# The top-k selection of a sparse-attention layer: a bound steered by counts in place of a search by bits

## The chip, the cores and the metric

The kernel runs on one core of a Trainium2 chip. A core has five engines with a queue each: TensorE (PE in the views, its weight loads PEld), VectorE (DVE), ScalarE (ACT), GpSimd (POOL) and SyncE (SP), which here issues all the DMA transfers. Each engine runs its own list of instructions in order and waits on semaphores for the others. The metric is the device time of one execution in microseconds, lower being better.

## The reference

The reference computes one decoder layer on 1024 tokens of width 1024 in float32. The part around the change is the sparse branch. For each query token t and each key position s it forms an index score, keeps the 256 highest-scored positions at or before t, and attends to those alone:

```python
dots = einsum('bqhd,bsd->bqhs', iq, ik) * IDX_DIM ** -0.5
score = einsum('bqh,bqhs->bqs', iw, relu(dots))        # 8 index heads
score = where(causal, score, NEG_INF)
_, idx = lax.top_k(score, 256)                         # ties: lowest position first
sel = c_kv[idx]                                        # then softmax attention, 8 heads, over sel
```

Beside it stand a projection of the input to all queries, keys and values, a sliding-window attention (8 heads), a cross attention over 256 memory tokens whose keys and values are two projections of the memory, a 4096-wide squared-ReLU network, and four layer norms. A token before position 256 has no more than 256 candidates, so it keeps them all and needs no selection.

## The kernel before

Tokens are handled in eight blocks of 128, a token to a partition. Every large product is made of three single-pass products of split operands: a value is rounded to a high part and the rest is kept as a low part, so each weight piece costs a rounding copy (`wh`, L156 on GpSimd, L158 on VectorE, L160 on ScalarE) and a subtraction (`wl`, L161) before TensorE can use it. `wload` loads and splits such pieces of 128x512, in a ring of four buffers each for raw, high and low.

Order of the stages: norm and transposition of the input, index queries and scores, then two things side by side, and then the attention of both branches, the output projection, the cross attention, the network and the final norm. The two things side by side are the ones that the change touches:

- The selection. Blocks 2 to 7 need one, with rows of 384 to 1024 scores (`sc`, 4224 columns over the six blocks). A score's bits are read as an ordered integer key of two 16-bit halves: `to_keys` makes the high keys as soon as a block's last index head is added (L584 to L597), and `search` finds the 256th largest key bit by bit, 15 steps on the high halves, then 16 on the low ones. In a step `look` counts a row's keys at or above the bound c, and `move` makes two one-column operations that halve the bracket (L665, L667). Blocks 2 to 5 are counted on VectorE (L584); blocks 6 and 7 on ScalarE, as a sum of signs (L680, with L684 and L687). The steps of the blocks are interleaved. Five passes of VectorE over each block (L733 to L737) then turn the threshold into a mask written over the scores, with a running sum that settles ties.
- The `fill` list: 53 units of TensorE work that need no selection, and seven that open the attention's memory and start its first loads. The first 36 are 18 units of projections of window and sparse queries and keys, mixed with 18 small ones (memory transposition, latent keys, the first memory keys); then come the memory keys (`mem_k`), the memory values (`mem_v`) and their product with the output weights (`mem_vo`). Memory weights are split on ScalarE, VectorE and GpSimd for the keys (`both`), on ScalarE and GpSimd alone for the values. A projection unit evicts its result on ScalarE (L393), splits it on GpSimd (L395, L396) and stores it (L398).

In the program text the whole selection stands ahead of the fill list. Earlier text has the higher priority; a planner orders each engine's list at compile time with estimated costs, so that fill units go between the steps of the selection where they are ready. `Pace` ties the fill matmuls to the last index-score matmuls by hand. At run time each list is fixed. The attention units that follow read the masks (L860), make probabilities (L863, L865), transpose and split them (`PT`, L768, L769) and multiply by the values (`VV`, L829, L830).

Of the kernel before, what the change touches and what calls it, by code (L numbers as in the profile page):

```python
# [21 lines left out]
P = 128  # L22
# [7 lines left out]
BUCKETS = 32  # L30
NOSYNC = mybir.DependencyInfo(mybir.DependencyClass.NoSync, mybir.DependencyReason.DATA)
# [3 lines left out]
def kernel(ctx: ExitStack, tc: tile.TileContext, x, mem, ln_emb_g, ln_emb_b, w_in, b_in,  # L35
# [240 lines left out]

    TW = 328
# [62 lines left out]
    bias_rows()  # L340
    st0.close()
# [217 lines left out]
    hi_k = {}  # L559
    HI = {7: (3, 0), 3: (7, 1024), 6: (4, 0), 4: (6, 896), 5: (2, 0), 2: (5, 768)}  # L560
    NQ = NB - 2
    cnt0, neg, flip, low, least, T_hi, base, need, t_lo = (
        p1.tile([P, NQ], F32, name=nm) for nm in ("cnt0", "neg", "flip", "low", "least", "T_hi", "base", "need", "t_lo"))

# [3 lines left out]
    def hi_half(n):  # L568
        mate, o = HI[n]
        if (n, mate) not in hi_k:  # L570
            hi_k[n, mate] = hi_k[mate, n] = p1.tile([P, 1536], I16, name="hi_k", tag="qs", bufs=4)
        hi_k[n] = hi_k[n, mate][:, o:o + (n + 1) * P]
        return hi_k[n]

    def col(t, n):
        return t[:, n - 2:n - 1]

    junk = {}

    def new_junk():  # L580
        junk["v"] = p1.tile([P, 1024], BF, name="junk", tag="r", bufs=3)

    def count(key, c, o, op=OP.is_ge):
        DVE.tensor_scalar(junk["v"][:, :key.shape[-1]], key, c, None, op0=op, op1=OP.add, accum_out=o)  # L584
# [3 lines left out]


    def to_keys(n):  # L590
        new_junk()
        count(halves(n, 1, I16), 0.0, col(cnt0, n))
        DVE.tensor_scalar(col(neg, n), col(cnt0, n), float(TOPK), -1.0, op0=OP.is_ge, op1=OP.add)
        DVE.tensor_scalar(col(flip, n), col(neg, n), 2.0, 1.0, op0=OP.mult, op1=OP.add)
        POOL.tensor_scalar(hi_half(n), halves(n, 1, I16), col(flip, n), col(neg, n), op0=OP.mult, op1=OP.add)
        DVE.tensor_scalar(col(least, n), col(neg, n), col(cnt0, n), float(TOPK), op0=OP.mult, op1=OP.add)
        DVE.tensor_scalar(col(low, n), col(neg, n), -65535.0, None, op0=OP.mult)  # L597

    def index_scores(j, qs):
        for e in range(2):  # L600
            h = 2 * j + e
            for n in (2, 4, 6, 3, 5, 7):
# [17 lines left out]
                if h == 7:  # L620
                    to_keys(n)
# [10 lines left out]

    SIGN = (NB - 1, NB - 2)
    lo_k = {}
    for tag, bufs, ns in (("ikh", 1, (7, 6)), ("ikl", 1, (5, 4, 3)), ("qs", 4, (2,))):
        t = p1.tile([P, sum(n + 1 for n in ns) * P], U16, name="lo_k", tag=tag, bufs=bufs)
        o = 0
        for n in ns:  # L640
            lo_k[n] = t[:, o:o + (n + 1) * P]
            o += (n + 1) * P
    new_junk()
    junk_a = p1.tile([P, 1024], BF, name="junk_a", tag="r", bufs=3)

    def srow(n):
        return sc[:, SCO[n]:SCO[n] + (n + 1) * P]

    class Counter:

        def __init__(self, n, key, least, out, bits):
            self.n, self.key, self.least, self.out, self.bits = n, key, least, out, bits
            self.c = self.small("c")
            DVE.memset(self.c, float(1 << bits - 1))

        def small(self, nm):
            return p1.tile([P, 1], F32, name=nm + str(self.n), bufs=2)

        def look(self):
            self.got = self.small("n")  # L660
            count(self.key, self.c, self.got)
# [78 lines left out]
    for unit, *args in fill:  # L740
        unit(*args)
# [680 lines left out]
```

## Time and profile before

| | |
|---|---|
| median of 3 runs | 1568.49 us (1567.64 to 1571.1) |
| the profiled execution | 1567.31 us, its span 1565.2 us |
| TensorE busy | 1436.3 us, 92% of the span |
| VectorE, GpSimd, ScalarE busy | 1166.9, 839.5, 797.0 us |
| mean granted TensorE clock | 0.966 |

The profile is one execution. Times inside it count from the first instruction, and the span ends with the last; the execution's own time is 2.1 us longer. Matmuls are pipelined, so a busy TensorE need not be at its peak, and the granted clock of a stretch says how fast it was let run. In a wait, the engine named last is the one whose work came last by the profile.

### The profile page before, as it was taken

To read this page: it belongs to the slowest core of one execution; us is meant where nothing else is said; L and a number is where in the kernel's file an instruction comes from. 1 tells how busy PE (TensorE), PEld (TensorE's weight loads), DVE (VectorE), ACT (ScalarE), POOL (GpSimd) and SP (SyncE) were. 2 spreads that over 40 slices of the span, in tenths; PEclk is the share of its full clock that TensorE was granted. 3 is DMA by queue.
4 is the path that set the end of the run, shared out by engine and by line. 5 is a ranking of instruction groups with operands and counts; after the bars stand their busy time and mean duration, and the time that the engine had idled before them with its cause. 6 is when DMAs were issued, how large, how long until landed. Compare 5 with 4: busy or idle time off the path is not lost. (4 is left out here: it accounts for less than half of the span.)

```text
span 1565.2 us, 22294 instructions
## 1 busy us (share of the span) xinstructions
PE 1436.3 (92%) x7190; PEld 1210.2 (77%) x7190; DVE 1166.9 (75%) x2442; ACT 797.0 (51%) x1665; POOL 839.5 (54%) x754
## 2 busy tenths in 40 slices
PE   5989997785998999899999979999999999999787
PEld 4877786764897988688888858888888877888676
DVE  8739899969786878985264495575544899988857
ACT  6336677673787875235334254545554533444422
POOL 6213855555556554755564675645444344453745
PEclk9999999896999999999999989999999999999999
DMA  6262444774649249623322133433333933420002
GB/s 218 72 163 71 135 135 139 234 249 108 199 144 247 95 135 290 181 94 114 109 73 90 41 108 122 136 107 126 117 126 114 389 110 109 148 69 1 27 28 107
DMA packets 139907, 206.63 MB, mean 132 GB/s; under 512 B 18055, under 2 KB 83086, under 8 KB 139790
## 3 DMA queue, kind: packets, MB, share of 16 engines
q1 hardware_dynamic: 139790, 205.21, 41.7%
q8 instruction: 57, 0.93, 0.3%
q14 instruction: 60, 0.49, 0.1%
HBM read 151.66 MB, written 52.45 MB: 130 GB/s over the span
## 5 line engine op out<-in xcount | busy, mean ns | idle before, releaser
L86 PE MATMUL b<-a,wh 128*128 128x512 f32 x1072 | 293.8, 396 | 9.0 <-DVE a L1077 8.2
L161 POOL TENSOR_TENSOR wl<-wr,wh 128x512 fp32r<-128x512 f32 x158 | 225.2, 1443 | 142.8 <-ACT wh L160 129.2
L86 PE MATMUL b<-wl,wh 128*128 128x512 f32 x1192 | 280.4, 395 | 15.1 <-POOL wl L1091 12.9
L86 PEld LDWEIGHTS b<-wl,wh 128*128 128x128 f32 x1192 | 226.1, 190 | 66.4 <-POOL wl L1091 15.8
L86 PEld LDWEIGHTS b<-a,wh 128*128 128x128 f32 x1072 | 203.7, 191 | 52.7 <-issue 9.0
L1091 POOL TENSOR_TENSOR wl<-a,wl 128x512 fp32r<-128x512 f32 x44 | 92.6, 2105 | 113.5 <-ACT wl L1090 109.1
L160 ACT ACTIVATE wh<-wr 128x512 fp32r<-128x512 f32 x136 | 81.3, 627 | 125.9 <-PE b L86 46.4
L1091 POOL TENSOR_TENSOR wh<-row,wh 128x512 fp32r<-128x512 f32 x72 | 97.9, 1366 | 84.4 <-ACT wh L1090 81.0
L86 PE MATMUL fill<-xT,wh 128*128 128x512 f32 (+1 forms) x416 | 125.5, 381 | 6.7 <-ACT wt L393 6.7
L86 PE MATMUL b<-wh,a 128*128 128x512 f32 (+1 forms) x416 | 120.9, 365 | 7.1 <-DVE a L761 5.3
L86 PE MATMUL b<-a,wl 128*128 128x512 f32 x400 | 120.7, 391 | 0.0
L1090 ACT ACTIVATE wh<-a 128x512 fp32r<-128x512 f32 x80 | 50.5, 631 | 115.2 <-PE b L86 83.8
L86 PEld LDWEIGHTS fill<-xT,wh 128*128 128x128 f32 x416 | 77.5, 192 | 22.7 <-ACT wt L393 8.2
L86 PEld LDWEIGHTS b<-wh,a 128*128 128x128 f32 x416 | 76.3, 191 | 21.0 <-DVE a L761 5.8
L1284 DVE TENSOR_TENSOR xr<-xr,b 128x512 f32<-128x512 f32 x132 | 81.6, 681 | 12.8 <-PE b L86 12.8
L86 PEld LDWEIGHTS b<-a,wl 128*128 128x128 f32 x400 | 75.2, 188 | 15.1
L1102 ACT ACTIVATE lt<-lt,colst 128x512 f32<-128x512 f32 x60 | 43.2, 722 | 73.7 <-DVE lt L1209 73.0
L86 PE MATMUL fill<-xT,wl 128*128 128x512 f32 (+1 forms) x208 | 78.8, 381 | 0.0
L769 DVE TENSOR_TENSOR PT<-tr,PT 128x512 fp32r<-128x512 f32 (+3 forms) x128 | 70.6, 576 | 9.0 <-ACT PT L768 8.7
L86 PE MATMUL b<-wl,a 128*128 128x512 f32 (+1 forms) x208 | 75.4, 365 | 1.7 <-POOL wl L161 1.7
L768 ACT ACTIVATE PT<-tr 128x512 fp32r<-128x512 f32 (+3 forms) x128 | 61.6, 507 | 26.1 <-PE tr L870 10.9
L1209 DVE TENSOR_TENSOR lt<-b,lt 128x512 f32<-128x512 f32 x80 | 53.2, 685 | 26.9 <-PE b L86 20.8
(328 smaller groups left out, 3664.2 us busy)
## 6 DMA issues: line engine op xcount, KB each, us to landing
row<-in_w_up_dram SPq DMA_DIRECT2D x32, 512.0 KB, 4.3
ff_d<-lt SPq DMA_DIRECT2D x28, 512.0 KB, 3.0
a<-in_w_down_dram SPq DMA_DIRECT2D x50, 256.0 KB, 5.4
a<-ff_d SPq DMA_DIRECT2D x46, 256.0 KB, 3.3
wr<-in_xa_wkv_dram SPq DMA_DIRECT2D x32, 256.0 KB, 3.9
wr<-in_w_o_dram SPq DMA_DIRECT2D x32, 256.0 KB, 3.1
wr<-in_xa_wq_dram SPq DMA_DIRECT2D x32, 256.0 KB, 3.0
wr<-vwo_d SPq DMA_DIRECT2D x32, 256.0 KB, 2.8
```

Source lines behind the costliest of these rows:

```text
L86: i = PE.matmul(o, a, b, start=start, stop=stop)
L160: ACT.activation(hs, raw, AF.Copy)
L161: lo[i % len(lo)].tensor_tensor(out=ls, in0=raw, in1=f(hs), op=OP.subtract)
L768: ACT.activation(PT[0], pt, AF.Copy)
L769: DVE.tensor_tensor(out=PT[1], in0=pt, in1=f(PT[0]), op=OP.subtract)
L1090: ACT.activation(hl[:, 0], raw, AF.Copy)
L1091: return lo.tensor_tensor(out=hl[:, 1], in0=raw, in1=f(hl[:, 0]), op=OP.subtract)
L1102: ACT.activation(c, src, AF.Relu, bias=colst[:, C_UP + col:C_UP + col + 1])
L1209: DVE.tensor_tensor(out=o, in0=a, in1=b, op=op)
L1284: DVE.tensor_tensor(out=xs, in0=xs, in1=p, op=op)
```

## The change

The search by bits is replaced, and where the selection stands in the text changes.

- `normal_bounds` computes once, for each row, the bound at which a normal distribution would have 251.5 scores above it, and the slope of that bound with the count.
- `Counter` and `Signer` take the place of `to_keys`: mean and variance of the first part of a row (at most 512 scores), a square root on GpSimd, and a first bound. Eight steps follow in place of 31. In each, the row's scores at or above the bound are counted in float32 (VectorE for blocks 2 to 5, ScalarE's signs for 6 and 7) and the bound moves by the miss times the slope times a weight from `PULL`.
- A last count marks the scores above the bound for all six blocks; marked scores are pushed far down and one instruction takes the eight largest of the rest. The needed one among them (the 256th less those counted) is the threshold, and the number of larger ones settles ties.
- A row whose count ended outside the eight is odd. The largest oddness of a partition goes by a transfer of 128 values into one row, VectorE takes its maximum, loads it into a register and branches: if any row is odd, all six blocks are done by bits on VectorE (`settle`), each instruction waiting for the one before it; if none is, that code is jumped over.
- The branch and the masks stand in the text between the 26th and the 27th fill unit, ahead of the last projection weight load, where all the selection stood ahead of the first.
- The weights of the memory values are split on three engines, as those of the keys are.

```diff
+PULL = (1.0, 0.8, 0.6, 0.9, 0.5, 0.3, 0.6, 0.25)
+WANT = TOPK - 4.5
+LAST = -2.0 ** 100
...
+    NQ = NB - 2
+    zc, zn, gp, gn = (pers.tile([P, NQ], F32, name=nm) for nm in ("zc", "zn", "gp", "gn"))
+    pull = pers.tile([P, len(PULL)], F32, name="pull")
+    turn8 = pers.tile([P, 1, 8], F32, name="turn8")
+    half_up = pers.tile([P, 1], F32, name="half_up")
+    def normal_bounds():
...
+        a, b, c = (p0.tile([P, NQ], F32, name=nm) for nm in ("za", "zb", "zd"))
+        DVE.tensor_copy(a, pos)
+        DVE.reciprocal(a, a)
+        DVE.tensor_scalar(b, a, WANT, None, op0=OP.mult)
+        DVE.tensor_scalar(c, a, -WANT, 1.0, op0=OP.mult, op1=OP.add)
+        for t in (b, c):
+            POOL.tensor_tensor(out=t, in0=t, in1=ex[:, 0:1].to_broadcast([P, NQ]), op=OP.pow)
+        DVE.tensor_tensor(out=c, in0=c, in1=b, op=OP.subtract)
+        DVE.tensor_scalar(zc, c, 1 / 0.1975, None, op0=OP.mult)
+        DVE.tensor_scalar(zn, zc, -1.0, None, op0=OP.mult)
+        DVE.tensor_tensor(out=b, in0=zc, in1=zc, op=OP.mult)
+        DVE.tensor_scalar(b, b, 0.5, None, op0=OP.mult)
+        POOL.tensor_tensor(out=b, in0=ex[:, 1:2].to_broadcast([P, NQ]), in1=b, op=OP.pow)
+        DVE.tensor_tensor(out=b, in0=b, in1=a, op=OP.mult)
+        DVE.tensor_scalar(gp, b, math.sqrt(2 * math.pi), None, op0=OP.mult)
+        DVE.tensor_scalar(gn, gp, -0.5, None, op0=OP.mult)
...
+    normal_bounds()
...
-            both = c < KT
+            both = True
...
+    CUT = 26
...
-    def to_keys(n):
-        new_junk()
-        count(halves(n, 1, I16), 0.0, col(cnt0, n))
-        DVE.tensor_scalar(col(neg, n), col(cnt0, n), float(TOPK), -1.0, op0=OP.is_ge, op1=OP.add)
-        DVE.tensor_scalar(col(flip, n), col(neg, n), 2.0, 1.0, op0=OP.mult, op1=OP.add)
-        POOL.tensor_scalar(hi_half(n), halves(n, 1, I16), col(flip, n), col(neg, n), op0=OP.mult, op1=OP.add)
-        DVE.tensor_scalar(col(least, n), col(neg, n), col(cnt0, n), float(TOPK), op0=OP.mult, op1=OP.add)
-        DVE.tensor_scalar(col(low, n), col(neg, n), -65535.0, None, op0=OP.mult)
...
+    class Counter:
+        def __init__(self, n):
+            self.n = n
+            self.own = p1.tile([P, 20], F32, name="own%d" % n)
+            self.way = p1.tile([P, 6], F32, name="way%d" % n)
+            self.turn = [0, 0, 0]
+            w = min(512, n * P)
+            st, mv, sd = (self.own[:, a:b] for a, b in ((0, 6), (6, 8), (8, 9)))
+            DVE.bn_stats(st, srow(n)[:, :w])
+            DVE.bn_aggr(mv, st)
+            POOL.tensor_tensor(out=sd, in0=mv[:, 1:2], in1=half_up, op=OP.pow)
+            self.begin(mv, sd)
+        def small(self, nm):
+            k = "cnu".index(nm)
+            self.turn[k] += 1
+            i = 2 * k + self.turn[k] % 2
+            return self.way[:, i:i + 1]
+        def begin(self, mv, sd):
+            self.c, g, self.rate = self.small("c"), self.own[:, 9:10], self.own[:, 12:20]
+            DVE.tensor_scalar(self.c, sd, col(zc, self.n), mv[:, 0:1], op0=OP.mult, op1=OP.add)
+            DVE.tensor_scalar(g, sd, col(gp, self.n), None, op0=OP.mult)
+            DVE.tensor_scalar(self.rate, pull, g, None, op0=OP.mult)
+        def look(self):
+            self.got = self.small("n")
+            s = srow(self.n)
+            DVE.tensor_scalar(junk["v"][:, :s.shape[-1]], s, self.c, None, op0=OP.is_ge, op1=OP.add, accum_out=self.got)
+        def move(self, i):
+            u, o = self.small("u"), self.small("c") if i < len(PULL) - 1 else col(bound, self.n)
+            DVE.tensor_scalar(u, self.got, WANT, self.rate[:, i:i + 1], op0=OP.subtract, op1=OP.mult)
+            DVE.tensor_scalar(o, u, self.c, None, op0=OP.add)
+            self.c = o
...
+    class Signer(Counter):
+        def begin(self, mv, sd):
+            self.c, g, self.rate = self.small("c"), self.own[:, 9:10], self.own[:, 12:20]
+            self.even = self.own[:, 10:11]
+            DVE.memset(self.even, (self.n + 1) * P - 2 * WANT)
+            DVE.tensor_scalar(self.c, sd, col(zn, self.n), mv[:, 0:1], op0=OP.mult, op1=OP.subtract)
+            DVE.tensor_scalar(g, sd, col(gn, self.n), None, op0=OP.mult)
+            DVE.tensor_scalar(self.rate, pull, g, None, op0=OP.mult)
+        def look(self):
+            self.got = self.small("n")
+            s = srow(self.n)
+            ACT.activation(junk["a"][:, :s.shape[-1]], s, AF.Sign, bias=self.c, accum_out=self.got)
...
-                    to_keys(n)
+                    every[n] = (Signer if n in SIGN else Counter)(n)
...
+    last = None
+    for i in range(len(PULL)):
+        for n in range(NB - 1, 1, -1):
+            s = every[n]
+            s.look()
+            if n in SIGN:
+                s.move(i)
+                continue
+            if last is not None:
+                last[0].move(last[1])
+            last = s, i
...
+    for n in ORDER:
+        over[n] = p1.tile([P, 1024], BF, name="over", tag="qs", bufs=4)
+        DVE.tensor_scalar(over[n][:, :(n + 1) * P], srow(n), col(bound, n), None, op0=OP.is_ge, op1=OP.add, accum_out=col(base, n))
+    DVE.tensor_scalar(need, base, -1.0, float(TOPK), op0=OP.mult, op1=OP.add)
+    odd, odd1 = p1.tile([P, NQ], F32, name="odd"), p1.tile([P, 1], F32, name="odd1")
+    DVE.tensor_scalar(odd, need, -4.5, None, op0=OP.add)
+    DVE.tensor_tensor(out=odd, in0=odd, in1=odd, op=OP.mult)
+    DVE.tensor_reduce(out=odd1, in_=odd, op=OP.max, axis=AX.X)
+    DVE.tensor_scalar(odd1, odd1, 16.0, None, op0=OP.is_gt)
+    odd_row = p1.tile([P, 1024], F32, name="odd_row", tag="r", bufs=3)[:1, :P]
+    SP.dma_start(odd_row, odd1)
+    some = p1.tile([1, 1], I32, name="some")
+    for i, n in enumerate(ORDER):
+        w = (n + 1) * P
+        v = p1.tile([P, 1024], F32, name="v", tag=("ikh", "ikl")[i % 2], bufs=1)
+        DVE.scalar_tensor_tensor(v[:, :w], over[n][:, :w], LAST, srow(n), op0=OP.mult, op1=OP.add)
+        DVE.max(m8[:, n - 2], v[:, :w])
+    DVE.tensor_reduce(out=some, in_=odd_row, op=OP.max, axis=AX.X)
+    sel = p1.tile([P, NQ, 8], F32, name="sel")
+    def each(t):
+        return t.rearrange("p (n o) -> p n o", o=1).to_broadcast([P, NQ, 8])
+    DVE.tensor_tensor(out=sel, in0=turn8.to_broadcast([P, NQ, 8]), in1=each(need), op=OP.is_equal)
+    DVE.tensor_tensor(out=sel, in0=sel, in1=m8, op=OP.mult)
+    DVE.tensor_reduce(out=thr, in_=sel, op=OP.add, axis=AX.X)
...
-    for n in range(2, NB):
-        POOL.tensor_scalar(lo_k[n], halves(n, 0), col(flip, n), col(low, n), op0=OP.mult, op1=OP.add)
-    search(hi_k, least, T_hi, 15)
-    for n in range(NB - 1, 1, -1):
-        count(hi_k[n], col(T_hi, n), col(base, n), OP.is_gt)
-        DVE.scalar_tensor_tensor(lo_k[n], hi_k[n], col(T_hi, n), lo_k[n], op0=OP.is_equal, op1=OP.mult)
-        DVE.tensor_scalar(col(need, n), col(base, n), -1.0, col(least, n), op0=OP.mult, op1=OP.add)
-    search(lo_k, need, t_lo, 16)
...
+    def by_bits(key, most, least, o, bits, a, go, scratch):
+        go(DVE.memset(a[0], float(1 << bits - 1)))
         for b in range(bits - 1, -1, -1):
+            go(DVE.tensor_scalar(scratch, key, a[0], None, op0=OP.is_ge, op1=OP.add, accum_out=a[1]))
+            go(DVE.tensor_scalar(a[1], a[1], least, float(1 << b), op0=OP.is_ge, op1=OP.mult))
+            go(DVE.tensor_scalar(a[0], a[1], a[0], -float(1 << b) / 2 if b else -1.0, op0=OP.add, op1=OP.add))
+        go(DVE.tensor_copy(o, a[0]))
+        go(DVE.tensor_scalar(scratch, key, o, None, op0=OP.is_gt, op1=OP.add, accum_out=most))
...
+    def go(i):
+        if done_[0]:
+            i._wait_ge(order, done_[0])
+        i.then_inc(order, 1)
+        done_[0] += 1
+    def settle(n):
         w = (n + 1) * P
+        hk, lk, jk = (t[:, :w] for t in bits_t)
+        cnt0, neg, flip, low, least, T_hi, b0, nd, t_lo, x, y, g = (sm[:, i:i + 1] for i in range(12))
+        go(DVE.tensor_scalar(jk, halves(n, 1, I16), 0.0, None, op0=OP.is_ge, op1=OP.add, accum_out=cnt0))
+        go(DVE.tensor_scalar(neg, cnt0, float(TOPK), -1.0, op0=OP.is_ge, op1=OP.add))
+        go(DVE.tensor_scalar(flip, neg, 2.0, 1.0, op0=OP.mult, op1=OP.add))
+        go(DVE.tensor_scalar(hk, halves(n, 1, I16), flip, neg, op0=OP.mult, op1=OP.add))
+        go(DVE.tensor_scalar(least, neg, cnt0, float(TOPK), op0=OP.mult, op1=OP.add))
+        go(DVE.tensor_scalar(low, neg, -65535.0, None, op0=OP.mult))
+        go(DVE.tensor_scalar(lk, halves(n, 0), flip, low, op0=OP.mult, op1=OP.add))
+        by_bits(hk, b0, least, T_hi, 15, (x, y), go, jk)
+        go(DVE.scalar_tensor_tensor(lk, hk, T_hi, lk, op0=OP.is_equal, op1=OP.mult))
+        go(DVE.tensor_scalar(nd, b0, -1.0, least, op0=OP.mult, op1=OP.add))
+        by_bits(lk, g, nd, t_lo, 16, (x, y), go, jk)
+        lo_i, hi_i = smi[:, 0:1], smi[:, 1:2]
+        go(DVE.tensor_scalar(x, t_lo, flip, low, op0=OP.mult, op1=OP.add))
+        go(DVE.tensor_copy(lo_i, x))
+        go(DVE.tensor_scalar(x, T_hi, flip, neg, op0=OP.mult, op1=OP.add))
+        go(DVE.tensor_scalar(hi_i, x, 65536.0, None, op0=OP.mult))
+        go(DVE.tensor_tensor(out=col(thr, n).bitcast(I32), in0=lo_i, in1=hi_i, op=OP.bitwise_or))
+        go(DVE.tensor_scalar(col(ngt, n), g, nd, None, op0=OP.subtract))
...
+    def settle_all():
+        rest = nc.values_load(some, [mybir.EngineType.DVE], min_val=0, max_val=1)
+        with tc.tile_critical():
+            with nc.If(rest > 0):
+                for n in range(2, NB):
+                    settle(n)
+    def mask_rows():
...
-    for unit, *args in fill:
+    for unit, *args in fill[:CUT]:
+        unit(*args)
+    settle_all()
+    mask_rows()
+    for unit, *args in fill[CUT:]:
```

## Rows read from the trace of the kernel before

**Rows 1.** Page, first part: busy us (share of the span) and instructions, each engine.
```profile
PE 1436.3 (92%) x7190; PEld 1210.2 (77%) x7190; DVE 1166.9 (75%) x2442; ACT 797.0 (51%) x1665; POOL 839.5 (54%) x754
```

**Rows 2.** Stretches: length; PE, PEld, DVE, ACT, POOL busy (instructions); clock, DMA share, GB/s.
```profile
163.50:224.00 60.50, 59.25 (x265) 48.32 (x266) 56.35 (x224) 52.30 (x133) 44.11 (x49) 1.00 0.52 147
224.00:241.00 17.00, 12.24 (x54) 9.76 (x52) 16.80 (x54) 5.53 (x14) 5.41 (x5) 0.94 0.34 100
...
258.00:346.00 88.00, 68.18 (x398) 58.72 (x399) 76.19 (x255) 59.06 (x142) 46.12 (x39) 0.90 0.74 234
346.00:400.00 54.00, 36.09 (x211) 33.02 (x210) 50.24 (x112) 22.85 (x66) 27.47 (x34) 0.75 0.43 113
400.00:580.00 180.00, 167.61 (x1232) 155.47 (x1231) 143.47 (x503) 142.47 (x376) 109.73 (x174) 0.98 0.58 173
```

**Rows 3.** TensorE's waits, 240 to 400 us: total, times, longest us.
```profile
PE mm L86 <- DVE PT L769: 8.1, 1, 8.1
PE fill L86 <- DVE wl L161: 8.0, 6, 2.2
...
PE fill L86 <- ACT wt L393: 4.9, 1, 4.9
PE fill L86 <- POOL wl L161: 4.3, 5, 1.9
PE lg L86 <- DVE sm L860: 3.4, 2, 3.2
PE mm L86 <- DVE wt L466: 2.3, 1, 2.3
PE mm L86 <- DVE VV L830: 2.0, 1, 2.0
```

**Rows 4.** VectorE in order of time: start us, us, instruction, idle time before it.
```profile
180.52 1.00 DVE L584 TENSOR_SCALAR_CACHE_REDUCE junk<-hi_k,c 128x768 bf16<-128x768 int16 x1
...
184.43 1.00 DVE L584 TENSOR_SCALAR_CACHE_REDUCE junk<-hi_k,c 128x768 bf16<-128x768 int16 x1
...
335.21 0.21 DVE L690 TENSOR_SCALAR t_lo<-u,c 128x1 f32<-128x1 f32 x1 [9.15 <-ACT u L684]
...
386.35 1.21 DVE L769 TENSOR_TENSOR PT<-tr,PT 128x256 fp32r<-128x256 f32 x3
```

**Rows 5.** VectorE's groups, 163 to 339 us: count, busy us, mean ns, idle before.
```profile
L584 DVE TENSOR_SCALAR_CACHE_REDUCE junk<-lo_k,c 128x768 bf16<-128x768 uint16 (+1 forms) x64 | 51.2, 801 | 0.0
...
L667 DVE TENSOR_SCALAR c<-u,c 128x1 f32<-128x1 f32 x116 | 23.4, 202 | 0.0
...
L161 DVE TENSOR_TENSOR wl<-wr,wh 128x512 fp32r<-128x512 f32 x11 | 10.6, 973 | 0.1
L158 DVE CAST wh<-wr 128x512 fp32r<-128x512 f32 x8 | 6.7, 841 | 0.1
```

**Rows 6.** ScalarE's groups, 163 to 339 us.
```profile
L680 ACT ACTIVATE junk_a<-lo_k,c 128x1024 bf16<-128x1024 uint16 (+1 forms) x32 | 34.8, 1088 | 11.3 <-DVE lo_k L711 11.3
```

**Rows 7.** VectorE's groups, 338 to 388 us: the five mask passes over six blocks.
```profile
L734 DVE TENSOR_TENSOR_SCAN r<-r,ngt 128x384 f32<-128x384 f32 (+5 forms) x6 | 10.2, 1697 | 0.1
L736 DVE SCALAR_TENSOR_TENSOR r<-r 128x384 f32<-128x384 f32 (+5 forms) x6 | 5.9, 986 | 0.0
L737 DVE TENSOR_TENSOR sc<-r 128x384 f32<-128x384 f32 (+5 forms) x6 | 5.8, 970 | 0.1
L735 DVE TENSOR_SCALAR r<-sc,thr 128x384 f32<-128x384 f32 (+5 forms) x6 | 5.5, 919 | 0.0
L733 DVE TENSOR_SCALAR r<-sc,thr 128x384 f32<-128x384 f32 (+5 forms) x6 | 5.0, 828 | 0.0
```

**Rows 8.** Page, DMA queues: packets, MB, their time of 16 engines' span.
```profile
q8 instruction: 57, 0.93, 0.3%
```

**Rows 9.** GpSimd's groups, 258 to 350 us.
```profile
L161 POOL TENSOR_TENSOR wl<-wr,wh 128x512 fp32r<-128x512 f32 x26 | 34.8, 1350 | 34.9 <-ACT wh L160 31.5 <-DMA wr<-in_xa_wkv_dram 3.4
```

**Rows 10.** GpSimd in order of time, beside the masks.
```profile
373.26 3.02 POOL L161 TENSOR_TENSOR wl<-wr,wh 128x512 fp32r<-128x512 f32 x1
```

More of the change, by code (lines that the diff above doesn't have):

```diff
@@ L558, with srow @@
     score_mm = []
[L559 to L563, printed above, removed]
+    SIGN = (NB - 1, NB - 2)
+    bound, base, need, thr, ngt = (p1.tile([P, NQ], F32, name=nm) for nm in ("bound", "base", "need", "thr", "ngt"))
+    def srow(n):
+        return sc[:, SCO[n]:SCO[n] + (n + 1) * P]
@@ new lines, with move @@
+    class Signer(Counter):
[10 more added lines that the diff above has]
+            ACT.activation(junk["a"][:, :s.shape[-1]], s, AF.Sign, bias=self.c, accum_out=self.got)
+        def move(self, i):
+            u = self.small("u")
+            ACT.activation(u, self.got, AF.Identity, bias=self.even)
+            if i < len(PULL) - 1:
+                o = self.small("c")
+                ACT.activation(o, u, AF.Identity, scale=self.rate[:, i:i + 1], bias=self.c)
+                self.c = o
+            else:
+                v = self.own[:, 11:12]
+                DVE.tensor_scalar(v, u, self.rate[:, i:i + 1], self.c, op0=OP.mult, op1=OP.add)
+                DVE.tensor_scalar(col(bound, self.n), v, -1.0, None, op0=OP.mult)
@@ L599, in index_scores @@
+    junk, every = {}, {}
     def index_scores(j, qs):
@@ L631 @@
     index_scores(*ahead)
[L635 to L661, printed above, removed]
-        def move(self, b):
-            u = self.small("u")
-            DVE.tensor_scalar(u, self.got, self.least, float(1 << b), op0=OP.is_ge, op1=OP.mult)
-            o = self.small("c") if b else self.out
-            DVE.tensor_scalar(o, u, self.c, -float(1 << b) / 2 if b else -1.0, op0=OP.add, op1=OP.add)
-            self.c = o
@@ L692, in search @@
-    def search(keys, least, out, bits):
-        every = [(Signer if n in SIGN else Counter)(n, keys[n], col(least, n), col(out, n), bits) for n in range(NB - 1, 1, -1)]
-        last = None
-        for b in range(bits - 1, -1, -1):
-            for s in every:
-                s.look()
-                if isinstance(s, Signer):
-                    s.move(b)
-                    continue
-                if last is not None:
-                    last[0].move(last[1])
-                last = s, b
-        last[0].move(last[1])
@@ L739 @@
-    behind["PE"] = [Pace(score_mm, 45, 1.2)]
-    for unit, *args in fill:
+    for k in ("v", "a"):
+        junk[k] = p1.tile([P, 1024], BF, name="junk", tag="r", bufs=3)
+    last = None
[9 more added lines that the diff above has]
+            last = s, i
+    last[0].move(last[1])
@@ new lines @@
+    m8 = p1.tile([P, NQ, 8], F32, name="m8")
+    ORDER = (2, 3, 4, 5, 6, 7)
+    over = {}
+    for n in ORDER:
[4 more added lines that the diff above has]
+    DVE.tensor_scalar(odd, need, -4.5, None, op0=OP.add)
@@ new lines @@
+    DVE.tensor_reduce(out=some, in_=odd_row, op=OP.max, axis=AX.X)
[5 more added lines that the diff above has]
+    DVE.tensor_reduce(out=thr, in_=sel, op=OP.add, axis=AX.X)
+    DVE.tensor_tensor(out=sel, in0=m8, in1=each(thr), op=OP.is_gt)
```

81 lines of the change are left out of this document (29 added, 52 removed).

## The prediction

> **What bounds the kernel now.** I read the page's first part first: TensorE is busy for 92% of the span [rows 1], so this is a TensorE kernel and a faster VectorE buys something only where TensorE waits for it. The second view is the stretches, cut where the top-k begins, halts and ends [rows 2]. From 163.5 to 224 us TensorE has nothing to gain (59.25 of 60.5 us busy). It then idles 4.8 us in 224 to 241, 19.8 us in 258 to 346 and 17.9 us in 346 to 400, while VectorE is busy for 87 to 99% of each of these; from 400 on TensorE is back at 93%. The granted clock, a mean over its two levels of 2.4 GHz (1.0) and 1.2 GHz (0.5), is 0.90 and 0.75 in the two long stretches, behind the idle times, and 0.98 afterwards, so part of "busy" there is slow matmuls: 68.18 x 0.10 = 6.8 us and 36.09 x 0.25 = 9.0 us.
>
> The third view, TensorE's waits from 240 to 400 us, names who was late [rows 3]: VectorE for 23.8 us in the five rows shown (8.1 + 8.0 + 3.4 + 2.3 + 2.0), ScalarE's eviction of a projection for 4.9 us, GpSimd's low halves for 4.3 us. The VectorE waits of the attention start (8.1, 3.4, 2.3, 2.0: 15.8 us) are ready probabilities, logits and values standing in VectorE's queue behind mask passes; the 8.0 us are weight splits standing behind counts. So the top-k, though it computes nothing for the matmuls before the attention, holds the queue that feeds them.
>
> **What the change removes.** The search now takes 15 + 16 = 31 counts per block. The row of one step to the same row of the next, 180.52 to 184.43, is 3.91 us for the four blocks that VectorE counts [rows 4]; 31 x 3.91 = 121 us, and the groups agree (the low keys' 64 counts are 51.2 us, the high keys' 60 are alike, and each has two small operations at 0.20 us behind it) [rows 5]. ScalarE's two blocks cost 1.09 us a pass [rows 6], and VectorE idles 9.15 us for their last step before the masks can begin [rows 4]. With eight steps VectorE spends 8 x 3.91 = 31 us: 90 us leave. A step's two small operations stay two. GpSimd's two key passes per block go as well.
>
> Counting now reads float32 scores instead of 16-bit keys. One count of 768 keys takes 1.00 us [rows 4]; less the 0.20 us of a one-column operation [rows 5] that is 1.04 ns a column, so the 16-bit form was no faster than one column per nanosecond, and a float32 comparison over all six blocks is 5.5 us in L735 [rows 7], 4224 columns at about the same pace. I take 0 and keep +6 us (a fifth of 31) as the upper bound; a gain is excluded to within the same 6 us by L733 at 5.0.
>
> **What it adds on VectorE.** After the search, six counts that also write the marks (5.5 to 5.9 us by a float32 pass over all six blocks, L735 and L736 [rows 7]), six multiply-adds that push marked scores away (5.9 us, as L736), six maxima of eight. No row shows the maximum; a cheap pass over the six blocks is 5.0 us and the scan 10.2 us [rows 7]; I take 5.9, the nearest plain pass. Some twelve small operations at 0.20 us are 2.5 us. Together 20 us, bounds 18 to 25. The masks themselves stay: 10.2 + 5.9 + 5.8 + 5.5 + 5.0 = 32.4 us [rows 7]. Starting at 163.5 us, the chain is 31 + 20 + 32 = 83 us, so it would end at 247 us if alone, and at about 265 us with the weight splits that lie between. Before it ends at 386.35 us, where the first probabilities follow it [rows 4]. About 120 us early is far more than TensorE can use: the masks are no longer late for anything.
>
> Each block's start (statistics of a first part of the row, a power on GpSimd, a few columns) takes the place of a count with four small operations and a GpSimd pass; I take 0, bounds -6 and +6 us (one pass a block). The constants of normal_bounds are some 30 operations of at most eight columns, 6 us at 0.20 us each over two engines; nothing needs them before the first block is scored: 0, at most +6.
>
> **What it adds as waits.** The missed-row flag goes out over SP's queue as one small transfer that waits for VectorE, and the weight loads behind it on SP wait too. VectorE then waits for its return, with the six maxima (12 us with their multiply-adds) between. No row shows this; the nearest is the 4.9 us that TensorE stood because ScalarE's queue was held [rows 3]. 0 to +5 us; I take 2. The branch makes VectorE skip about 890 instructions (six blocks of some 114, and the accumulator reads). An instruction packet takes 0.003 x 16 x 1565.2 / 57 = 1.3 us of one DMA engine by the page [rows 8], so one to four of them are 1.3 to 5 us on VectorE; behind it stand the masks and the splits, and the slack of 120 us hides it: 0. The Trainium skill, "Runtime: NRT & Kernel Launch", section "Instruction fetch mechanics", says that a taken branch to a page not held must wait for its fetch; no run shown here has a branch, so the trace neither confirms nor denies it.
> The branch also parts the program: work traced after it stays behind work traced before it in every queue, and the cut falls ahead of the last of the five projection weight loads. 0 to 4.8 us (the idle time around such a changeover in 224 to 241 [rows 2]); I take 2.
>
> **What moves.** The masks move from 346 to 386 us to about 215 to 265, beside GpSimd's splits of the last projection and first memory weights. Beside the masks a GpSimd split took 3.02 us [rows 10] where the 26 of the stretch before took 1.35 [rows 9]. I charge two such splits' excess, 3 us, with 0 and 15 us as ends (none, or all of the eight pieces slowed by 1.7 us and the two passes before them). The Trainium skill, "Advanced Engine Details and Errata", section "VectorE Performance Modes", says that a VectorE instruction in a two-port mode and GpSimd block each other; by that the eleven microseconds of L733 and L735 would be the part that stops GpSimd, and the charge would be at most 11 us. The row agrees that the two engines slow each other there.
>
> **The memory weights.** The value half has 32 pieces of 128x512; 16 of them move: VectorE gets 16 x (0.84 + 0.97) = 29 us [rows 5], GpSimd loses 16 x 1.35 = 22 us of the 34.8 us it has in this stretch [rows 9]. VectorE has the room only because 90 us left it; without that, these 29 us would stand in front of the masks. It shortens the 4.3 us that TensorE waits for GpSimd; I take 2.
>
> **The sum.** 224 to 241: the 4.9 us go (ScalarE stood for the change from high to low keys, which no longer exists). 258 to 346: the 8.0 us of VectorE, 2 of GpSimd, and half of the 6.8 us of clock: 13. Its transfers allow it: at a DMA share of 1 instead of 0.74 the same bytes need 65 of the 88 us. 346 to 400: 15.8 us and half of 9.0: 20. Together 38 us. Against it 2 us (flag), 2 us (boundary), 3 us (GpSimd beside the masks), and 3 us because what is late next, the loads of keys and queries on SP, takes a part of the attention start: 28 us. From the profiled execution's 1567.3 us (span 1565.2 and 2.1 around it) that is 1539.3; the median of the runs shown is 1.2 us above that execution, so 1540.
>
> **Rivals.**
> A. TensorE stays fed by loads and GpSimd from 258 to 346, and nothing is won there: for it, the DMA share is already 0.74, and GpSimd is idle for half of the stretch [rows 2] and yet late by 4.3 us [rows 3], so its inputs come late; against it, the largest wait in the group is for VectorE. What remains is the attention start less what the loads keep: about 13 us, 1555. Chance 0.22.
> B. All idle time and clock of the three stretches come back: 42.5 + 15.8 = 58 us; less the 7 us of flag, boundary and GpSimd, 1516. Against it, no other stretch runs without idle time (7% in 400 to 580). Chance 0.08.
> C. The attention starts no sooner: its loads are queued where they were, and the 28 us turn into waits for them. Only the 4.9 us are won and the boundary takes them: about 1568, no change. Chance 0.08.
> D. The bound misses rows and the branch is not skipped. Then VectorE runs 31 serial steps for each of six blocks: 0.92 us for the mean count (5.5 us over six blocks, L735 [rows 7]) and twice 0.20 us is 1.32 us; x 31 x 6 = 246 us, with four more passes a block about 270 us in which nothing else runs on VectorE, and TensorE needs its splits: 1540 + 270 = 1810. It decides as soon as one of 768 rows ends outside 1 to 8 needed keys. For it: eight corrections from a normal guess, and scores that are sums of eight rectified terms. Against it: if a row's density is r times the guess, the miss shrinks by the product of |1 - a r| over the eight weights a, which is 0.045 at r = 0.5, below 0.001 at 1.5, 0.04 at 3: a first miss of 70 keys still ends within 4. Chance 0.10.
>
> **How the numbers follow.** The forecast has 0.52, with a range of its own of 1528 to 1552 (the added-cost bounds of some +20 us half hidden, the clock terms either way). Faster by over 0.2% (3.1 us, about what a measurement tells from no change) is forecast, A and B: 0.82; within it C: 0.08; slower D: 0.10. The range 1520 to 1568 takes in the forecast, A and most of C, and leaves out D and half of B.
>
> **What would show it.** Right: some 8 counts per block; the last mask pass before about 280 us; no TensorE wait for VectorE's probabilities at the first attention units; the clock near 1 there; the projection wait of 4.9 us gone. Wrong: masks on time and TensorE still idle by 20 us between 258 and the attention, with waits for weights (A) or for keys and queries (C); VectorE solid with one-column steps for hundreds of us (D); a VectorE gap of over 10 us at the branch that TensorE repeats.

## The result, and the profile after

The changed kernel took 1555.85 us (median of 4 runs, 1552.96 to 1557.56) beside 1569.8 of the kernel before in the same series: ratio 0.9916, 95% interval 0.9894 to 0.9938. That is 13 to 14 us won, about half of the 28 forecast. The profiled execution, 1557.56 us, is the slowest of the four; its span is 1555.8.

The selection did get shorter, as the page's first part shows (compare [rows 1]): VectorE and ScalarE lose 63 and 65 us of work. TensorE's busy time rises by 7 us, although it does the same work.

```profile
PE 1442.9 (93%) x7190; PEld 1205.6 (77%) x7190; DVE 1104.3 (71%) x2076; ACT 732.5 (47%) x1475; POOL 826.5 (53%) x756
```

The stretches say where it counted [rows 2]. First the one stretch of before that the rows above leave out, 241 to 258 us, and then the kernel after (columns as there):

```profile
241.00:258.00 17.00, 16.32 (x68) 13.29 (x68) 16.93 (x56) 16.24 (x42) 14.54 (x15) 0.86 0.48 136
```
```profile
224.00:241.00 17.00, 17.00 (x75) 13.67 (x74) 6.29 (x12) 3.28 (x5) 13.62 (x15) 1.00 0.60 170
241.00:258.00 17.00, 7.84 (x37) 6.28 (x35) 16.96 (x13) 3.97 (x6) 14.21 (x11) 0.81 0.39 109
258.00:346.00 88.00, 72.64 (x446) 63.64 (x447) 52.59 (x57) 26.58 (x51) 39.33 (x31) 0.88 0.76 243
346.00:400.00 54.00, 48.10 (x340) 44.80 (x340) 39.14 (x145) 36.77 (x100) 29.02 (x52) 0.94 0.66 184
```

The idle time of 224 to 241 is gone, and the attention start (346 to 400) has 12 us more of TensorE at a clock of 0.94 instead of 0.75. But 241 to 258 lost 8.5 us that it had before. TensorE's waits, 240 to 400 us, name the place [rows 3]:

```profile
PE fill L91 <- DVE wh L163: 15.0, 1, 15.0
PE fill L91 <- ACT wh L165: 3.9, 3, 2.4
PE fill L91 <- DVE wl L166: 3.3, 2, 2.1
...
PE mm L91 <- DVE PT L868: 0.3, 1, 0.3
```

The 8.1 us that the first probabilities waited are down to 0.3, as forecast, and one new wait of 15.0 us, for the cast of a weight on VectorE, stands at the top. VectorE in order of time shows who it was [rows 4]:

```profile
228.29 0.27 DVE L756 TENSOR_REDUCE some<-odd_row 1x1 int32<-1x128 f32 x1 [3.01 <-DMA odd_row<-odd]
236.13 0.17 DVE L822 TENSOR_SCALAR ngt<-ngt 128x6 f32<-128x6 f32 x1 [7.56 <-DMA kb_d<-wt]
...
261.37 2.07 DVE L829 TENSOR_TENSOR_SCAN pre<-r,ngt 128x896 f32<-128x896 f32 x1
263.37 0.39 DVE L163 CAST wh<-wr 128x512 fp32r<-128x512 f32 x1
```

VectorE stands idle 3.0 us for the flag and 7.6 us at the branch (the row names a transfer as what ended that; the rows of the branch instruction, further down, show that it was the branch), then runs the masks as one row from 236 us on, and the cast of a memory-key weight (L163), which TensorE needs from 248.8 us on (the cast's end at 263.8 less the wait of 15.0), stands behind 27 us of them. SyncE's queue stands too, since its next weight load needs a raw buffer that this cast must first read:

```profile
SPq L157 <- DVE wh L163: 19.0, 1, 19.0
```

The second loss is in a stage that the change doesn't touch. From 960 to 1200 us both kernels run the network's first product without a gap and at full clock; the stage after it, 1240 to 1400, is shown as well. Before, then after:

```profile
960.00:1200.00 240.00, 240.00 (x1061) 198.76 (x1060) 140.18 (x183) 123.16 (x204) 124.75 (x93) 1.00 0.36 119
1240.00:1400.00 160.00, 156.96 (x683) 128.56 (x682) 152.30 (x224) 67.69 (x118) 75.28 (x44) 0.99 0.40 136
```
```profile
960.00:1200.00 240.00, 240.00 (x1031) 193.50 (x1031) 128.66 (x170) 122.90 (x199) 117.35 (x88) 1.00 0.35 115
1240.00:1400.00 160.00, 156.99 (x683) 128.49 (x682) 148.61 (x220) 67.90 (x118) 75.23 (x44) 0.99 0.32 109
```

240 us held 1061 matmuls before and hold 1031 now: one in 226 ns against one in 233, with TensorE busy all the time and the clock at 1.00 in both. In the later stage the counts are equal. The timeline has the same in single rows, of before and of after: nine matmuls whose starts are (2.20 - 0.39) / 8 = 226 ns apart, seven with (1.80 - 0.40) / 6 = 233 (0.39 to 0.40 us is one matmul from start to end).

```profile
1101.14 2.20 PE L86 MATMUL b<-a,wh 128*128 128x512 f32 x9
```
```profile
1099.63 1.80 PE L91 MATMUL b<-a,wh 128*128 128x512 f32 x7
```

What differs there is where the operands lie. The change adds seven small lasting tiles (224 bytes a partition with their padding), and every later buffer of that pool's side of SBUF moves by 224 = 3 x 64 + 32 bytes. Before, nearly all operands of 512-column matmuls start at 32 modulo 64. After, most activations (`xT`, `a`) start at 0 and weights (`wh`, `wl`) still at 32; by the built programs' lists of buffers, 2736 of the 512-column matmuls now have a moving and a stationary operand whose starts differ by 32 modulo 64, against 96. In 1240 to 1400 both operands are weight buffers, and nothing moved. A start at 0 is not slow by itself: some matmuls of the kernel after's last stage have activations as both operands, both starting at 0, and there the starts of the matmuls are (2.88 - 0.39) / 11 = 226 ns apart.

```profile
1524.54 2.88 PE L91 MATMUL po<-a,a 128*128 128x512 f32 x12
```

### The profile page after: what moved, and what is told of

Its sections match the earlier page's. It is cut to its first block, busy times and chain, and to the rows that moved or that the text cites. A ratio compares the mean times of both kernels' runs of the same rounds, so it can differ in the third digit from the quotient of the medians.

```text
span 1555.8 us, 21768 instructions
## 1 busy us (share of the span) xinstructions
PE 1442.9 (93%) x7190; PEld 1205.6 (77%) x7190; DVE 1104.3 (71%) x2076; ACT 732.5 (47%) x1475; POOL 826.5 (53%) x756
## 5 line engine op out<-in xcount | busy, mean ns | idle before, releaser
L91 PE MATMUL b<-a,wh 128*128 128x512 f32 x1072 | 300.5, 402 | 8.8 <-DVE a L1176 8.1
L166 POOL TENSOR_TENSOR wl<-wr,wh 128x512 fp32r<-128x512 f32 x150 | 217.9, 1471 | 141.3 <-ACT wh L165 133.3
L165 ACT ACTIVATE wh<-wr 128x512 fp32r<-128x512 f32 x128 | 76.0, 627 | 140.7 <-PE b L91 46.3
L1308 DVE TENSOR_TENSOR lt<-b,lt 128x512 f32<-128x512 f32 x80 | 53.4, 686 | 37.2 <-PE b L91 32.4
L1189 ACT ACTIVATE wh<-row 128x512 fp32r<-128x512 f32 x72 | 45.0, 627 | 66.8 <-PE b L91 52.2
```

The source lines that it names most:

```text
L91: i = PE.matmul(o, a, b, start=start, stop=stop)
L165: ACT.activation(hs, raw, AF.Copy)
L166: lo[i % len(lo)].tensor_tensor(out=ls, in0=raw, in1=f(hs), op=OP.subtract)
L1189: ACT.activation(hl[:, 0], raw, AF.Copy)
L1308: DVE.tensor_tensor(out=o, in0=a, in1=b, op=op)
```

## The experiments

Two questions: is the slower pace the placement, and what is the row of masks worth. The times of before beside them are 1568.08, 1569.71 and 1569.74 us in the three series.

**Placement.** Three kernels: the change shifted by another 32 bytes, so that the starts agree again; the kernel before shifted by 32; the change shifted by 64.

```diff
     half_up = pers.tile([P, 1], F32, name="half_up")
+    shift = pers.tile([P, 8], F32, name="shift")    # 64 bytes: [P, 16]
+    POOL.memset(shift, 0.0)
```

> The changed kernel plus one unused 32-byte column block in the lasting buffers, so that every later buffer on that side of SBUF starts 32 bytes further; nothing else differs. Theory (placement): the change's seven small lasting tiles moved these buffers by 224 bytes, so that 2640 512-column matmuls more than before have a moving operand and a stationary operand whose starts differ by 32 bytes modulo 64; their starts stand 233 ns apart in the trace after (1031 matmuls in 960 to 1200 us), against 227 before (1061). With the shift undone 1061 per 240 us come back there, and up to 2640 x 6.5 ns = 17 us are won: 1539 to 1544 us against 1555.85. Rival (the 233 ns were the state of that execution or chip, not the kernel): 1553 to 1558, as after, whatever the pace in its trace. Rival (the slower pace is caused by what the change does on VectorE or GpSimd): pace stays 233, time as after.

> The kernel before plus the same unused 32-byte block, which puts its operands into the same mixed placement as those of the kernel after (2736 matmuls of 512 columns with starts 32 bytes apart modulo 64, against 96). Nothing else differs. Theory (placement): slower by 12 to 17 us, 1582 to 1587 against 1569.8; about 1031 matmuls in 240 us of the up stage instead of 1061. Rivals (state of the execution; or a cause in the top-k's code): no difference, 1567 to 1573, 1061 matmuls.

> The changed kernel with an unused block of 64 bytes in place of 32. Theory (what counts is the difference of the operands' starts modulo 64 bytes): the same 2736 matmuls of 512 columns stay mixed, about 1031 in 960 to 1200 us, and the time stays at 1553 to 1558. Rival (any move of these buffers helps, or it is a larger modulus that counts): 1061 matmuls and about 1541, as with 32 bytes, or a pace of its own.

Measured: the change with 32 bytes 1541.32 us (ratio to before 0.982, 0.9794 to 0.9846); the kernel before with 32 bytes 1579.77 (1.0066, 1.0042 to 1.0089); the change with 64 bytes 1554.97 (0.9907, 0.9871 to 0.9943). The stretch 960 to 1200 in the three, in this order:

```profile
960.00:1200.00 240.00, 240.00 (x1060) 198.72 (x1060) 135.33 (x180) 125.27 (x207) 117.23 (x88) 1.00 0.40 134
```
```profile
960.00:1200.00 240.00, 240.00 (x1034) 193.56 (x1033) 133.97 (x177) 123.40 (x200) 119.51 (x90) 1.00 0.35 116
```
```profile
960.00:1200.00 240.00, 240.00 (x1034) 193.49 (x1033) 128.34 (x170) 123.06 (x199) 115.93 (x87) 1.00 0.35 117
```

The pace follows the placement in both kernels, and so does the time: an unused 32-byte tile wins 14.5 us in one and costs 11.7 in the other (just under the 12 expected), a 64-byte one does nothing. That it is less than 17 us (2640 matmuls by 6.5 ns) may come from passes whose loss is hidden where TensorE waits anyway; no run shows that part. The rivals (the state of the execution, the code of the selection) are out.

**The row of masks.** All variants of the changed kernel from here on have the 32-byte shift, so 1541.3 us (0.982) is their mark. First the masks were asked for one block at a time behind every second later unit, and in another kernel all memory weights were kept off VectorE:

```diff
-    mask_rows()
-    for unit, *args in fill[CUT:]:
-        unit(*args)
+    for i, (unit, *args) in enumerate(fill[CUT:]):
+        unit(*args)
+        if i % 2 == 0 and i // 2 < NQ:
+            mask_rows([i // 2])      # one block
```
```diff
-            both = True
+            both = False
```

> The changed kernel with the 32-byte shift and with the six blocks' masks issued one at a time behind every second of the later projection units, instead of in one row of about 38 us. Theory (the row of masks holds the memory-key weight casts on VectorE): TensorE's wait of 15.0 us for the cast at 263.8 us goes, the granted clock of 241 to 280 stays near 1 (0.81 and 0.61 in the trace after), and the time is 8 to 15 us under that of the shifted kernel alone: 1526 to 1534. Rival (the weight transfers, or the queue that issues them, set the pace there): the wait moves to a DMA or to ScalarE's casts, and under 3 us are won. Rival (masks late): attention's first units wait for probabilities again, several us at 360 to 400.

> The changed kernel with the 32-byte shift and with all memory-key and memory-value weight splits on ScalarE and GpSimd, none on VectorE; the masks stand in one row as in the change. Theory (masks on VectorE block the casts): the 15.0 us wait goes too, but each pair of units now has four GpSimd differences of 1.47 us (3.31 beside the masks) against about 5.5 us of matmuls, so GpSimd is the next to be late: 0 to 8 us under the shifted kernel alone, TensorE's waits naming GpSimd's wl. Rival (weight transfers or their issue bind): waits stay, for a DMA, time within 3 us of the shifted kernel. Rival (the change to three engines is worth what the prediction gave it nothing for): slower by over 5 us.

The first told nothing of the masks: 1543.34 us (0.9832, 0.9809 to 0.9856), because the planner laid the passes into VectorE's list as before, in one row, and TensorE's wait stood unchanged:

```profile
PE fill L91 <- DVE wh L163: 15.6, 1, 15.6
```

The second did remove the wait, and won nothing: 1541.04 us (0.9835, 0.9809 to 0.986). (In its expectation, the 3.31 us beside the masks are two differences together, 1.66 us each.) TensorE's waits of 224 to 400 us in the shifted kernel, then in this one, and this one's GpSimd weight differences from 244 to 284 us:

```profile
PE fill L91 <- DVE wh L163: 15.8, 2, 15.6
PE fill L91 <- ACT wh L165: 4.8, 6, 1.5
PE fill L91 <- POOL wl L166: 1.7, 2, 0.8
```
```profile
PE fill L91 <- POOL wl L166: 9.7, 11, 3.9
PE fill L91 <- ACT wh L165: 9.3, 6, 2.6
```
```profile
L166 POOL TENSOR_TENSOR wl<-wr,wh 128x512 fp32r<-128x512 f32 x9 | 17.5, 1957 | 0.0
```

The 15.8 us went, and 12.5 came back: 8.0 more for GpSimd, 4.5 more for ScalarE. Beside the masks a GpSimd difference takes 1.96 us instead of 1.35 [rows 9], and the row of masks in turn takes 48.8 us (233.2 to 282.0) instead of 38.0 in the shifted kernel (234.8 to 272.8), though no splits stand in it any more. By these numbers each engine slows the other, so moving the splits to GpSimd replaces one late engine by another.

Four more kernels: without the branch; without the masks; the kernel before with the three-engine split alone; and the masks tied by hand, so that casts and masks really alternate.

```diff
-    settle_all()      # the kernel without the branch
-    mask_rows()       # the kernel without the masks
```
```diff
-            both = c < KT     # in the kernel before
+            both = True
```
```diff
# masks tied: wload keeps its last VectorE difference in last_split
-        if i % 2 == 0 and i // 2 < NQ:
-            mask_rows([i // 2])
+        if i % 2 == 0 and 2 <= i // 2 < NQ + 2:
+            with tc.issue_after(last_split[0].ins):
+                mask_rows([i // 2 - 2])
```

> The changed kernel with the 32-byte shift, without the branch and the serial code behind it (left out: the treatment of rows that the bound misses; the flag and its transfer stay). Theory (the branch costs): VectorE's gap of 7.6 to 8.0 us ahead of the first mask pass goes, the masks and with them the cast for which TensorE stood 15.6 us come 8 us sooner, and the time falls by 4 to 8 us from 1541.3 to 1533 to 1537. Rival (what TensorE wins at 245 to 280 is taken back by the weight and key transfers before the attention, as when the splits left VectorE): the gap goes and the time stays within 3 us of 1541.

> The changed kernel with the 32-byte shift, without the mask passes (left out: the scores are not masked; search, verification and branch stay, and the attention does the same work on unmasked scores). Theory (the row of masks on VectorE costs what TensorE waits there): the 15.6 us wait goes, and the time falls by 10 to 15 us to 1526 to 1531. Rival (the transfers before the attention take a lead back): the wait goes, the DMA share of 264 to 364 stays at 0.8 or above, TensorE waits for weight casts behind transfers instead, and the time falls by no more than 5 us, 1536 to 1542.

> The kernel before with one part of the change alone: the memory-value weights split on three engines; search, masks and placement as before. Theory of the prediction (it needs the room that the shorter search leaves): the 29 us more on VectorE stand ahead of the masks, which the attention awaits, and the time rises by 5 to 29 us, 1573 to 1597. Rival (GpSimd was the late one): faster by 2 to 4 us. Rival (no effect): within 3 us of 1568.

> The changed kernel with the 32-byte shift and with each block's mask passes tied by hand behind the memory-weight differences on VectorE that precede them in the text, so that casts and masks alternate in VectorE's list (asking for it by the place in the text alone had left the list as it was). Theory (masks hold the casts, and that costs time): TensorE's 15.6 us wait shrinks to under 6 us, the granted clock of 241 to 284 stays above 0.9, and the time falls to 1528 to 1535. Rival (a lead won there is taken back before the attention or behind it): the wait shrinks and the time stays at 1538 to 1543. Rival (masks now late): waits of several us for probabilities and logits at the first attention units, slower than 1543.

Without the branch: 1540.47 us (0.9816, 0.979 to 0.9842), not the 4 to 8 us less that the theory expected. The 8 us gap is gone from VectorE, whose mask passes begin at 222 us, while the flag still travels, and the time stays. The passes begin 13 us sooner but run slower, beside a GpSimd that is busy for 14.9 of the 17 us of 224 to 241, and the cast comes only 4 us sooner (257.9 instead of 262.0). TensorE still stands 12.8 us for it, and then waits 6.1 us for loaded keys where the shifted kernel waits 1.4:

```profile
257.92 0.41 DVE L163 CAST wh<-wr 128x512 fp32r<-128x512 f32 x1
```
```profile
PE fill L91 <- DVE wh L163: 13.6, 2, 12.8
PE lg L91 <- DMA wl<-kb_d: 3.4, 4, 1.4
...
PE lg L91 <- DMA wh<-kb_d: 2.7, 1, 2.7
```

Without the masks: 1527.09 us (0.9738, 0.9707 to 0.9769), 14.2 us under the mark; my rival, a lead that the transfers take back, is out. With the masks tied: 1527.91 us (0.974, 0.9705 to 0.9775), 13.4 us under the mark, and as fast as without any masks. This version beats both kernels. Its VectorE list alternates, its 241 to 258 us are full, its attention starts at full clock (346 to 400), and its waits (224 to 400 us) have no long one left:

```profile
255.96 0.98 DVE L838 TENSOR_TENSOR sc<-r 128x512 f32<-128x512 f32 x1
256.86 1.51 DVE L163 CAST wh<-wr 128x512 fp32r<-128x512 f32 x1
...
301.42 1.21 DVE L838 TENSOR_TENSOR sc<-r 128x1024 f32<-128x1024 f32 x1
```
```profile
241.00:258.00 17.00, 17.00 (x99) 14.98 (x98) 16.82 (x14) 4.43 (x7) 15.92 (x13) 1.00 0.83 228
258.00:346.00 88.00, 69.78 (x463) 62.71 (x461) 65.76 (x87) 32.82 (x72) 43.57 (x38) 0.94 0.89 263
346.00:400.00 54.00, 51.84 (x377) 47.72 (x376) 43.60 (x162) 42.70 (x120) 34.83 (x60) 1.00 0.56 168
```
```profile
PE fill L91 <- DVE wl L166: 4.7, 3, 3.4
PE fill L91 <- POOL wl L166: 4.2, 3, 3.0
PE fill L91 <- ACT wh L165: 3.6, 4, 1.6
PE fill L91 <- DVE wh L163: 2.4, 2, 2.0
```

The masks end at 302.6 us, 28 later than in the change as it stands, and the attention doesn't notice. What is left of 258 to 346 runs beside a DMA share of 0.89.

The three-engine split alone, in the kernel before: 1566.14 us (0.9973, 0.9957 to 0.9989), 2 to 7 us faster, where I had expected 5 to 29 slower.

**The branch taken.** The price of missed rows, in one run:

```diff
-    DVE.tensor_scalar(odd1, odd1, 16.0, None, op0=OP.is_gt)
+    DVE.tensor_scalar(odd1, odd1, -1.0, None, op0=OP.is_gt)
```

> The changed kernel with the 32-byte shift and with the flag's bound lowered, so that the branch is taken on every run and all six blocks are done again by bits, one instruction waiting for the other. The prediction's price for this case: 246 us of counts and small operations and some passes, about 270 us more, so 1811 us. If each instruction's wait for the one before it adds to the 0.20 us of a small operation, it is more: at 0.3 us more an instruction, some 850 instructions add 250 us, 2060. If TensorE's work goes on beside it for longer than the prediction held, less than 1811.

1850.76 us, 309 over the mark and 40 over the expected 1811. The serial code runs from 228 to about 555 us, and TensorE waits 328 us for one cast behind it (granted clock 0.51 in 240 to 540 us). TensorE's wait, the start of the serial code, and a step of the 1024-column block in it:

```profile
PE fill L91 <- DVE wh L163: 329.0, 2, 328.3
```
```profile
228.44 0.55 DVE L797 TENSOR_SCALAR_CACHE_REDUCE bits<-sc 128x384 bf16<-128x384 int16 x1 [3.66 <-DMA wr<-in_xa_wkv_dram]
...
543.71 1.28 DVE L775 TENSOR_SCALAR_CACHE_REDUCE bits<-bits,bits_sm 128x1024 bf16<-128x1024 uint16 x1
544.91 0.08 DVE L775 DVE_READ_ACCUMULATOR bits<-bits,bits_sm 128x1 f32 x1
545.03 0.21 DVE L776 TENSOR_SCALAR bits_sm<-bits_sm 128x1 f32<-128x1 f32 x1
545.28 0.21 DVE L777 TENSOR_SCALAR bits_sm<-bits_sm 128x1 f32<-128x1 f32 x1
545.53 1.28 DVE L775 TENSOR_SCALAR_CACHE_REDUCE bits<-bits,bits_sm 128x1024 bf16<-128x1024 uint16 x1
```

## Why the prediction was wrong, step by step

The step that failed is "The constants of normal_bounds ... nothing needs them before the first block is scored: 0, at most +6". I priced their operations and not their place: 14.5 us by the times, 15.1 by the ratios (0.9916 - 0.982 of 1569.8), for lasting tiles that the term put at nothing. With that undone the change takes 1541.32 us, against 1540 forecast; but this closeness is partly luck, since two parts of the sum were off in opposite directions: what was won, less flag, boundary and loads, was forecast as 38 - 7 = 31 us and is 40.8, and the masks' new place was charged 3 and costs 12.5.

Rival A's number, 1555, is the one that came out, but not for its reason, that nothing would be won from 258 to 346 us. Pairing the two kernels' matmuls by their order in time, the change is 14.0 us behind at 258 us of before and 3.6 ahead at 346; it is 22.4 ahead at 580 and loses 13 of that behind it, at the slower pace.

- **What was won, 38 us:** 40.8 by the tied version (0.026 of 1569.8), which has neither the placement's loss nor the row's. Its parts lie about where the prediction put them. Matmuls paired as above, the tied version gains 5.0 us in 224 to 241 of before (4.9 forecast: ScalarE's eviction), 4.3 in 241 to 258 (none), 8.5 in 258 to 346 (13) and 22.3 in 346 to 400 (20: the first probabilities, and the clock, 1.00 instead of 0.75).
- **The masks' new place, charged 3 us (0 to 15) for GpSimd:** 12.5 us by the ratios (0.982 - 0.974 of 1569.8), inside its bounds but for another reason. "The masks are no longer late for anything" looked at who waits for the masks. The cost came from what waits behind them, the casts in VectorE's own list; the prediction saw just that mechanism in the kernel before, for probabilities behind masks, and didn't ask it again after the move. The passes also take longer there, 37.9 us instead of 32.4 [rows 7], the scan most. The two passes that the prediction singled out as those that stop GpSimd, L733 and L735, took only 0.2 us more each; the other three, which read two tensors each, took 5.1 more:

```profile
L829 DVE TENSOR_TENSOR_SCAN pre<-r,ngt 128x384 f32<-128x384 f32 (+5 forms) x6 | 12.3, 2061 | 0.0
```

- **Flag, boundary and the next wait for loads, 2 + 2 + 3 us:** the kernel without the branch gives nothing back that can be told from zero, so the gap of 7.6 us cost TensorE nothing that shows, while it stood for the row of masks in any case. The flag's 3.0 us, the boundary and the transfers' 3 us were not measured by themselves.
- **The branch, 1.3 to 5 us on VectorE:** the gap at it is 7.6 to 8.2 us when the code is jumped over and 3.7 when it is run, so the jump adds some 4 us. VectorE's branch instruction, in the kernel after and in the one that runs the code, shows the same: 4.4 us lie between its end and the first mask pass at 236.13, 0.1 between its end and the serial code at 228.44.

```profile
L816 DVEq COMPARE_BRANCH  x1: 63/63/63, 231.7 to 231.7; - x1
```
```profile
L818 DVEq COMPARE_BRANCH  x1: 56/56/56, 228.3 to 228.3; - x1
```

The Trainium skill, "Runtime: NRT & Kernel Launch", section "Instruction fetch mechanics", has a taken branch wait for the fetch of its target. The traces agree: in the 4.4 us lies one 8 KB packet of the instruction queue q14 (starting at 233.9 us), in the 3.7 us gap of the other kernel none. That VectorE waits for just this packet is not shown.
- **The search, 31 steps to 8, float32 counts at the price of 16-bit ones:** right. The step is 3.91 us again [rows 4]:

```profile
173.73 1.00 DVE L648 TENSOR_SCALAR_CACHE_REDUCE junk<-sc,way 128x768 bf16<-128x768 f32 x1
177.64 1.00 DVE L648 TENSOR_SCALAR_CACHE_REDUCE junk<-sc,way 128x768 bf16<-128x768 f32 x1
```

- **The verification, 20 us (18 to 25):** 205.5 to 225.3 us, 20 us; the six maxima 5.3 instead of 5.9. The masks, forecast to end at about 265 us, end at 274: the first count of the search starts at 169.1 us instead of 163.5, the search ran 5 us longer than 8 x 3.91 (2.7 us of four splits among its steps, 1.5 of waiting for ScalarE), and the gaps came on top.
- **The memory weights, 2 us, and "VectorE has the room only because 90 us left it":** the gain is there (4 us alone, in the kernel before), but not for the reason that room was needed. Why it pays there stays open: TensorE's waits for GpSimd's low halves fall from 4.3 to 2.0 us, but those for VectorE's rise from 8.0 to 17.7, and the wait for the first probabilities falls from 8.1 to 1.2.
- **Rival D:** not met; no row was missed. Its price would have been 309 us, not 270: from one count to the next are 1.82 us for 1024 columns, 0.14 more than the count's 1.28 and twice 0.20; the accumulator read and the gaps between dependent instructions were left out (x 186 = 26 us). The other 13 us are not taken apart.
- **The test that I set** ("masks on time and TensorE still idle by 20 us between 258 and the attention") pointed too late by 10 us and to weights and loads, not to VectorE's own list.

## What to carry to other kernels

When a long piece of work moves to an earlier place on an engine, ask what stands behind it there, not only who waits for it, and let it alternate with what others need: here the alternation was worth 12.5 to 13.4 us, as much as the change had won as it stood. When the changed kernel is slower in a stage that nobody touched, count instructions per microsecond there before reading waits; if the pace differs at equal clock, compare the addresses of the operands. A new small lasting buffer is not free of effect: here 32 bytes were worth 12 to 15 us either way, so try padding such buffers until later ones keep their place modulo 64 bytes.

## What the runs showed of the hardware

A gap-free stream of single-pass 512-column matmuls at full clock ran at one in 226 to 227 ns where the moving and the stationary operand start at 32 modulo 64 bytes, and at one in 232 to 233 ns where one of them starts at 0; 32 bytes more reverse it in either direction, 64 (in the changed kernel) don't. With both at 0, twelve matmuls in a row ran at 226 ns in the kernel after and at (2.92 - 0.40) / 11 = 229 in the two others of this placement, so it is the difference of the starts that counts most. The Trainium skill, "SBUF — State Buffer", section "Who interferes with whom", gives TensorE two independent read ports for the two operands. A pace that depends on how the two starts lie to each other does not follow from that; the five kernels measure it, and do not show its cause. Which of the two operands is held, if either is, and whether every placement of 32 apart does it, stays open: where passes with equal and with unequal starts alternate, the trace after shows both at 231 to 234 ns. The starts of most 256-column matmuls stand 117 to 120 ns apart in either placement (medians).

Where a branch jumped over some 890 instructions, 4.4 us lay between its end and VectorE's next pass, against 0.1 us where it did not jump. Where VectorE's mask passes and GpSimd's 128x512 differences ran side by side, both took longer: 1.96 us a difference instead of 1.35, 48.8 us for the row of masks instead of 38.0.
